# Where the split weights begin in their buffers: one start for both parts, or one for each

## The chip, the cores and the metric

The kernel runs on one core of a Trainium2 chip. The metric is the device time of one execution in microseconds. Before the change it is 2129.86 us, the median of three runs (2129.07 to 2129.96).

## The reference

The reference computes a decoder trunk of two layers on 256 tokens of 2048 features, in float32. Layer 0 mixes tokens by MoBA attention (16 heads of 128; with 256 tokens there is one block of keys, so this is plain causal attention), layer 1 by multi-head latent attention (low-rank queries and keys/values, a shared rotary key). Each mixer is followed by a gated feed-forward part with a causal convolution of width 3 on the gate:

```python
def conv_glu_ffn(h, w_gate, w_up, conv_w, conv_b, w_down):
    g = h @ w_gate                                # 2048 -> 5632
    g = causal_depthwise_conv(g, conv_w, width=3) + conv_b
    return (jax.nn.silu(g) * (h @ w_up)) @ w_down # 5632 -> 2048

for i in range(2):
    x = x + mixer_i(rms_norm(x, attn_norm[i]))
    x = x + conv_glu_ffn(rms_norm(x, ffn_norm[i]), ...)
```

The weights are some 387 MB of float32; each is used once.

## The kernel before

**Tiling.** All weights are laid out on the host in the order of their use, as 370 units of four pieces; a piece is 128 partitions x 512 columns (288 in one projection). Each float32 operand is split into a high part in the type fp32r and a low part, what is left of it, and a product is made of three fp32r products: high x high, high x low, low x high. The pieces are consumed in 1480 steps, called quanta, one piece each.

There are two ways to use a piece:

- *By token* (`tok_major`, L238 to L240): the activations' columns are loaded into TensorE as weights, and the piece is streamed, 512 columns at a time, six matmuls a piece. This is used for the q, k and v projections of layer 0 (units 0 to 47, in four groups of twelve, one group for four heads, called the heads below) and for most projections of layer 1 (units 200 to 221).
- *By feature* (`feat_major`, L255 to L257): the piece is loaded into TensorE, 128 columns at a time, and 256 tokens of activations are streamed, twelve matmuls a piece, in triples. L255 is high weights x high activations, L256 high weights x low activations, L257 low weights x high activations. This is used for both output projections (units 48 to 63 and 222 to 237), gate/up and down of layer 0 (64 to 151 and 152 to 195), the first projection of layer 1 (196 to 199), and gate/up and down of layer 1 (238 to 325 and 326 to 369).

**Splitting.** `Stream.split` takes a raw piece that DMA has brought, lets ScalarE copy it into a buffer `whi` (L99) and VectorE subtract that copy from the raw piece into a buffer `wlo` (L100). There are five buffers of either kind, used in turn. A buffer has 512 + 64 floats in each partition, that is 2304 bytes, nine times 256. The part need not begin at the buffer's first byte: `starts(u, j)` gives, for piece j of unit u, at which float the high part begins and at which the low part. Eight floats are 32 bytes.

```python
b, c = self.starts(u, j)
hi = self.part_pool.tile([P, 512 + ROOM], F32R, name="whi")[:, b : b + 512]
lo = self.part_pool.tile([P, 512 + ROOM], F32R, name="wlo")[:, c : c + 512]
```

Before the change, high and low part of a piece begin at the same place: at 32 bytes where pieces are used by token, at 96 bytes where they are used by feature, and at 80 bytes in the first piece of certain units (`entries`) of the feature-major stages: every eighth unit in gate/up, every eleventh in down, and single ones in the output projections and in unit 197. The activations' tile `h` begins 32 bytes into its buffer.

**Order.** The order of the work is written out by hand: each quantum's matmuls, and a table of side work (norms, evacuations, attention heads) that is put in behind given quanta. TensorE's queue is therefore one fixed list. In gate/up and down it holds nothing but L255, L256 and L257. In the first unit of each gate/up, two pieces of work of the norm stand between the matmuls, behind the unit's third and fourth piece: the sums (`column_rstd`, L320) and two transposes that spread the result over the partitions (`spread_rows`, L330). Attention's transposes (L443, L503) and scores (L467) stand between matmuls in the heads, in layer 1's projections and in the output projections.

Of the kernel before, what the change touches and what calls it, by code (L numbers as in the profile page):

```python
# [45 lines left out]

ROOM = 64

BY_TOKEN, BY_FEATURE, ENTRY = 8, 24, 20

H_START = 8

# [58 lines left out]
def trunk(ctx: ExitStack, tc: tile.TileContext, a, out):  # L111
# [38 lines left out]
    units += units_of("ffn_down1")  # L150
    def starts(u, j):

        if u < 48 or 200 <= u < 222:
            return BY_TOKEN, BY_TOKEN
        b = ENTRY if j == 0 and u in entries else BY_FEATURE
        return b, b


    entries = {52, 56, 60, 197, 224, 226, 228, 230, 234}
    for first_unit, n, every in ((65, 87, 8), (152, 44, 11), (239, 87, 8), (326, 44, 11)):  # L160
        entries |= set(range(first_unit, first_unit + n, every))
    assert len(units) == 370
    ws = Stream(nc, raw_pool, part_pool, units, starts)


# [930 lines left out]
```

## Time and profile before

| what | value |
|---|---|
| median of three runs | 2129.86 us |
| profiled execution | 2129.42 us, its span 2127.6 us |
| TensorE busy | 2119.6 us, 100% of the span |
| VectorE, ScalarE busy | 1388.7 us (65%), 1140.9 us (54%) |
| granted clock | 1.0 |
| HBM | 387.01 MB read, 183 GB/s |

In a timeline, each row has the start of an instruction, its duration (that of a matmul is modelled, and matmuls overlap), the engine, the line, and out<-in. The distance between two starts is what TensorE really spends on a matmul. In a table of windows each row is one stretch of the span: the busy time and, in brackets, the number of instructions of each engine that lie in it or reach into it.

### The profile page before, as it was taken

The numbers are of one execution on the slowest core, as the hardware profiler recorded it, in microseconds if no ns is written. First come the engines' busy times: TensorE is split into PE (matmuls) and PEld (weight loads), VectorE is DVE, ScalarE is ACT, GpSimd is POOL, SyncE is SP. The second block draws the span as 40 slices with busy tenths as digits, with TensorE's granted clock in tenths as the row PEclk, the third lists the DMA queues.
The fourth block names the chain that finished last, engine by engine and source line by source line (L and its number), as shares of the span: only waits on it lengthen the run. The fifth ranks groups of instructions, "written<-read, shape, count | busy, mean of one in ns | idle before, by whom it ended". The sixth has DMA issues, their size and how long they took to land.

```text
span 2127.6 us, 42062 instructions
## 1 busy us (share of the span) xinstructions
PE 2119.6 (100%) x16683; PEld 2045.3 (96%) x16683; DVE 1388.7 (65%) x3035; ACT 1140.9 (54%) x2207; POOL 45.6 (2%) x37
## 2 busy tenths in 40 slices
PE   9999999999999999999999999999999999999999
PEld 7888889999999999999999789999999999999999
DVE  6776666766667666655556885766666666654554
ACT  6555555555555555555556675655555555544443
POOL 0000000000000000000000210000000000000000
PEclk9999999999999999999999999999999999999999
DMA  7455445555555555555555433555555555555553
GB/s 268 159 178 178 158 164 194 193 189 194 199 196 187 193 198 198 198 187 192 197 181 186 144 115 139 187 191 191 186 183 194 179 193 184 185 197 193 202 186 129
DMA packets 59381, 391.81 MB, mean 184 GB/s; under 512 B 6960, under 2 KB 10032, under 8 KB 13232
## 3 DMA queue, kind: packets, MB, share of 16 engines
q1 hardware_dynamic: 59040, 389.10, 51.4%
q8 instruction: 130, 2.13, 0.4%
q14 instruction: 67, 0.55, 0.1%
q10 hardware_dynamic: 144, 0.04, 0.0%
HBM read 387.01 MB, written 2.10 MB: 183 GB/s over the span
## 4 chain that ended last, share of the span: by engine, by line
PE 98%; DVE 1%; issue 0%; ACT 0%; POOL 0%; DMA 0%; SPq 0%; POOLq 0%; ACTq 0%
PE acc L256 26%; PE acc L255 26%; PE acc L257 26%; PE acc L239 5%; PE acc L238 5%; PE acc L240 5%; PE sc L467 1%; PE tp L443 1%; PE sc L514 1%; PE tp L503 0%; PE sc L470 0%; PE sc L515 0%; DVE wlo L100 0%; DVE junk L373 0%; POOL hr L386 0%
## 5 line engine op out<-in xcount | busy, mean ns | idle before, releaser
L100 DVE TENSOR_TENSOR wlo<-raw,whi 128x512 fp32r<-128x512 f32 (+1 forms) x1480 | 999.9, 683 | 436.4 <-ACT whi L99 434.4
L99 ACT CAST whi<-raw 128x512 fp32r<-128x512 f32 (+1 forms) x1480 | 878.7, 614 | 477.8 <-PE acc L256 328.0
L255 PE MATMUL acc<-h,whi 128*128 128x256 f32 x2880 | 802.7, 279 | 0.0
L256 PE MATMUL acc<-h,whi 128*128 128x256 f32 x2880 | 802.3, 279 | 0.0
L257 PE MATMUL acc<-h,wlo 128*128 128x256 f32 x2880 | 802.1, 279 | 0.0
L255 PEld LDWEIGHTS acc<-h,whi 128*128 128x128 f32 x2880 | 546.5, 190 | 0.0
L257 PEld LDWEIGHTS acc<-h,wlo 128*128 128x128 f32 x2880 | 540.8, 188 | 0.0
L256 PEld LDWEIGHTS acc<-h,whi 128*128 128x128 f32 x2880 | 540.7, 188 | 0.0
L256 PE MATMUL acc<-a,whi 128*128 128x256 f32 x1408 | 392.3, 279 | 0.0
L255 PE MATMUL acc<-a,whi 128*128 128x256 f32 x1408 | 392.3, 279 | 0.0
L257 PE MATMUL acc<-a,wlo 128*128 128x256 f32 x1408 | 392.2, 279 | 0.0
L255 PEld LDWEIGHTS acc<-a,whi 128*128 128x128 f32 x1408 | 267.3, 190 | 0.0
L257 PEld LDWEIGHTS acc<-a,wlo 128*128 128x128 f32 x1408 | 264.4, 188 | 0.0
L256 PEld LDWEIGHTS acc<-a,whi 128*128 128x128 f32 x1408 | 264.3, 188 | 0.0
L238 PE MATMUL acc<-whi,h 128*128 128x512 f32 (+1 forms) x448 | 176.0, 393 | 0.5 <-ACT whi L99 0.5
L239 PE MATMUL acc<-wlo,h 128*128 128x512 f32 (+1 forms) x448 | 170.0, 379 | 0.1
L240 PE MATMUL acc<-whi,h 128*128 128x512 f32 (+1 forms) x448 | 169.6, 379 | 0.0
L255 PE MATMUL acc<-oT,whi 128*128 128x256 f32 x512 | 145.0, 283 | 0.0
L256 PE MATMUL acc<-oT,whi 128*128 128x256 f32 x512 | 141.8, 277 | 0.0
L257 PE MATMUL acc<-oT,wlo 128*128 128x256 f32 x512 | 141.7, 277 | 0.0
L669 DVE TENSOR_TENSOR g<-acc,rstd_b 128x256 f32<-128x256 f32 x88 | 37.4, 425 | 131.0 <-PE acc L257 128.1
L676 ACT ACTIVATE c<-g,par 128x256 f32<-128x256 f32 x88 | 53.1, 603 | 110.2 <-DVE g L669 110.2
(146 smaller groups left out, 1737.5 us busy)
## 6 DMA issues: line engine op xcount, KB each, us to landing
raw<-in_ffn_gu SPq DMA_DIRECT2D x176, 1024.0 KB, 4.8
raw<-in_ffn_down SPq DMA_DIRECT2D x88, 1024.0 KB, 4.8
raw<-in_moba_wk SPq DMA_DIRECT2D x16, 1024.0 KB, 4.9
raw<-in_moba_wv SPq DMA_DIRECT2D x16, 1024.0 KB, 4.8
raw<-in_moba_wo SPq DMA_DIRECT2D x16, 1024.0 KB, 4.8
raw<-in_mla_wo SPq DMA_DIRECT2D x16, 1024.0 KB, 4.9
raw<-in_moba_wq SPq DMA_DIRECT2D x13, 1024.0 KB, 4.8
raw<-in_mla_wkv_a SPq DMA_DIRECT2D x8, 576.0 KB, 3.8
```

What stands on the lines that cost most here:

```text
L99: self.nc.scalar.copy(hi[:, :n], w)
L100: self.nc.vector.tensor_tensor(lo[:, :n], w, hi[:, :n].bitcast(F32), op=ALU.subtract)
L238: mm(o, hi, t_hi[:, :n], start=kt == 0, stop=False)
L239: mm(o, hi, t_lo[:, :n], start=False, stop=False)
L240: mm(o, lo, t_hi[:, :n], start=False, stop=kt == k_last)
L255: mm(o, w_hi, src[:, kt, :S], start=first and k == 0, stop=False, skip_group_check=True)
L256: mm(o, w_hi, src[:, kt, S:], start=False, stop=False, skip_group_check=True)
L257: mm(o, w_lo, src[:, kt, :S], start=False, stop=kt == k_last, skip_group_check=True)
L443: nc.tensor.transpose(tp[:, (i * NT + t) * P : (i * NT + t + 1) * P], flat[:, t, c : c + P], ident)
L467: mm(o, qT[:, i, q0 : q0 + P], kT[:, i, :n], start=True, stop=self.rope is None)
L669: nc.vector.tensor_tensor(self.g[:, 2:], self.gate["acc"][:, :S], self.norm.rstd_b, op=ALU.mult)
L676: nc.scalar.activation(self.c, self.g[:, 2:], AF.Identity, bias=par[:, cb : cb + 1], scale=self.cw(2))
```

## The change

The high part of a feature-major piece stays at 96 bytes; its low part moves from 96 to 224 bytes. The pieces at 80 bytes are gone: the first pieces of the `entries` units are now like all others. In the heads of layer 0, the four groups of twelve units get a pair each: (32, 32) as before in the first, (32, 160) in the second, (224, 96) in the third and (96, 224) in the fourth. Layer 1's token-major pieces stay at (32, 32). The order of instructions is the same on all engines.

```diff
-BY_TOKEN, BY_FEATURE, ENTRY = 8, 24, 20
+BY_TOKEN, BY_FEATURE = (8, 8), (24, 56)
+BY_HEADS = ((8, 8), (8, 40), (56, 24), (24, 56))
...
     def starts(u, j):
 
-        if u < 48 or 200 <= u < 222:
-            return BY_TOKEN, BY_TOKEN
-        b = ENTRY if j == 0 and u in entries else BY_FEATURE
-        return b, b
-
-
-    entries = {52, 56, 60, 197, 224, 226, 228, 230, 234}
-    for first_unit, n, every in ((65, 87, 8), (152, 44, 11), (239, 87, 8), (326, 44, 11)):
-        entries |= set(range(first_unit, first_unit + n, every))
+        if u < 48:
+            return BY_HEADS[u // 12]
+        return BY_TOKEN if 200 <= u < 222 else BY_FEATURE
+
```

## The prediction

> **What bounds the kernel now.** I read the page first (busy time, clock, chain), then the busy time of each engine by stage, then TensorE's timeline where two stages begin.
>
> ```profile
> span 2127.6 us, 42062 instructions
> PE 2119.6 (100%) x16683; PEld 2045.3 (96%) x16683; DVE 1388.7 (65%) x3035; ACT 1140.9 (54%) x2207; POOL 45.6 (2%) x37
> PE 98%; DVE 1%; issue 0%; ACT 0%; POOL 0%; DMA 0%; SPq 0%; POOLq 0%; ACTq 0%
> ```
>
> TensorE is busy all the time and is 98% of the chain that ended last. VectorE and ScalarE have a third and more to spare. So only two things can move the time: how many matmuls there are (the change leaves that alone) and how far apart their starts lie.
>
> The stages that matter are gate/up and down of both layers, in which nothing but weight matmuls runs. These are windows, gate/up from the norm's transposes on, down from its first matmul (busy time and count of PE, PEld, DVE, ACT, POOL, then clock, DMA share, GB/s): gate/up and down of layer 0, gate/up and down of layer 1, and heads 4 to 15 of layer 0.
>
> ```profile
> 398.95:872.90 473.95, 473.95 (x4178) 473.95 (x4177) 329.51 (x610) 254.57 (x482) 0.00 (x0) 1.00 0.55 195
> 872.90:1112.47 239.57, 239.57 (x2114) 239.57 (x2113) 135.74 (x223) 120.61 (x206) 0.00 (x0) 1.00 0.55 194
> 1382.97:1874.96 491.99, 491.99 (x4178) 491.99 (x4178) 329.68 (x610) 260.80 (x482) 0.00 (x0) 1.00 0.53 188
> 1874.96:2123.62 248.66, 248.66 (x2114) 248.66 (x2112) 124.09 (x190) 106.93 (x173) 0.00 (x0) 1.00 0.51 182
> 74.96:300.63 225.67, 225.26 (x1066) 187.08 (x1064) 153.08 (x477) 122.09 (x257) 11.80 (x6) 1.00 0.48 171
> ```
>
> Gate/up from there on is 348 pieces of 12 matmuls, 4176 in all (the count takes in the ones that the edges cut). They take 473.95 us in layer 0 and 491.99 in layer 1; the 176 pieces of down, 2112 matmuls, take 239.57 and 248.66. Code, shapes, starts and pieces at 80 are the same in both layers, TensorE never idles, the clock is 1.00. So there are **two prices** for one and the same matmul: 473.95 / 4176 = 113.5 ns, which I call fast, and 491.99 / 4176 = 117.8 ns, slow. Which one holds is settled at this entry and then lasts for all 524 pieces, through the change from gate/up to down. The entry of layer 0:
>
> ```profile
> 398.76 0.43 PE L330 MATMUL tp<-ident,rstd 128*128 128x128 f32 x2
> 398.95 0.36 PE L255 MATMUL acc<-h,whi 128*128 128x256 f32 x1
> 399.15 0.28 PE L256 MATMUL acc<-h,whi 128*128 128x256 f32 x1
> 399.27 0.28 PE L257 MATMUL acc<-h,wlo 128*128 128x256 f32 x1
> ...
> 400.44 0.28 PE L255 MATMUL acc<-h,whi 128*128 128x256 f32 x1
> ...
> 400.79 0.28 PE L255 MATMUL acc<-h,whi 128*128 128x256 f32 x1
> ```
>
> and of layer 1:
>
> ```profile
> 1382.97 0.36 PE L255 MATMUL acc<-h,whi 128*128 128x256 f32 x1
> 1383.17 0.28 PE L256 MATMUL acc<-h,whi 128*128 128x256 f32 x1
> 1383.29 0.28 PE L257 MATMUL acc<-h,wlo 128*128 128x256 f32 x1
> ...
> 1384.47 0.28 PE L255 MATMUL acc<-h,whi 128*128 128x256 f32 x1
> ...
> 1384.82 0.28 PE L255 MATMUL acc<-h,whi 128*128 128x256 f32 x1
> ```
>
> Read the first column. In both, the norm's two transposes (L330) break the stream, the first gap is 0.20, and the first piece, which is one at 80 bytes, takes 1.49 and 1.50 us. The next triple takes 0.35 us in both, and from there layer 0 goes on at 0.34 a triple (its window) and layer 1 stays at 0.354 a triple (its window). From the second matmul to the piece's end it is 1.29 us (399.15 to 400.44) against 1.30 (1383.17 to 1384.47): that 0.01 us is all in which the two entries differ.
>
> **The change, part by part.** The order of instructions is the same on all five engines, so no wait, queue or DMA moves. What changes is where reads of the weights begin.
>
> 1. *Pieces at 80 go.* At the fast price one costs, at the start of layer 0's down,
>
> ```profile
> 872.90 0.28 PE L255 MATMUL acc<-a,whi 128*128 128x256 f32 x1
> ...
> 874.31 0.28 PE L255 MATMUL acc<-a,whi 128*128 128x256 f32 x1
> ```
>
> 1.41 us for 12 matmuls against 12 x 0.1133 = 1.36: 0.05 us dearer, and it falls back to fast at once. Layer 0's gate/up holds 11 of them (0.55 us), its down 4 (0.20), the other feature-major stages 7 amid fast ones (0.35). Without them the fast price is (473.95 - 0.55) / 4176 = 113.4 ns, the entry's stall in it. At the slow price none of the 14 later pieces at 80 of layer 1 brought the fast price back, so nothing is lost there by taking them out.
>
> 2. *What the entry then looks like.* The first piece behind L330 becomes an ordinary one. For ordinary pieces (both parts at 96) that start behind transposes or sums there are 24 (in the output projections, unit 196 and the first unit of gate/up) whose first gap is 0.20 or 0.21. I followed the gaps of each: 20 settle at 0.113, most of them within four matmuls, and 4 stay at 0.118. The first of the 24, one of the four (from its second matmul), and the last (likewise):
>
> ```profile
> 302.48 0.37 PE L255 MATMUL acc<-oT,whi 128*128 128x256 f32 x1
> 302.68 0.28 PE L256 MATMUL acc<-oT,whi 128*128 128x256 f32 x1
> ...
> 303.60 0.28 PE L255 MATMUL acc<-oT,whi 128*128 128x256 f32 x1
> ```
>
> ```profile
> 1293.05 0.28 PE L256 MATMUL acc<-oT,whi 128*128 128x256 f32 x1
> ...
> 1293.99 0.28 PE L255 MATMUL acc<-oT,whi 128*128 128x256 f32 x1
> ```
>
> ```profile
> 1381.44 0.28 PE L256 MATMUL acc<-h,whi 128*128 128x256 f32 x1
> ...
> 1382.13 0.28 PE L256 MATMUL acc<-h,whi 128*128 128x256 f32 x1
> ```
>
> From the second matmul on, eight gaps take 0.92 us in the first (302.68 to 303.60), eight 0.94 in the second (1293.05 to 1293.99), six 0.69 in the third (1381.44 to 1382.13): fast, slow, fast. All three of the 24 that read the norm's output are fast, the last of them two microseconds ahead of layer 1's slow entry. If an ordinary piece opens the stage, fast is the likely state of each layer, at 20 in 24 if the low parts' new place does no harm. Layer 1 at the fast price: gate/up 491.99 - 473.40 = 18.6 us less; down, whose window holds 2111 gaps, 248.66 - 2111 x 0.1133 = 9.4 less.
>
> 3. *Low parts 128 bytes further on.* No row has a high and a low part at different starts, so this price is unknown. What bears on it: a buffer is 2304 bytes, nine times 256, so consecutive pieces alternate by 256 bytes modulo 512, and the settled spacing in the windows does not; a move by 256 is free. A move by 16 (the pieces at 80) costs 0.05 us a piece. 128 lies between. Its ends: nothing (0.1133 a matmul), and every feature-major piece at the 1.41 of the piece at 80, which is also the slow price. I take nothing, since 128 keeps the place within 128 bytes, and 80 does not keep the place within 64; the other end stays as a rival.
>
> 4. *Heads of layer 0.* In these stages the weights are the streamed side (512 columns), and in the last three groups the pairs move one part or both. Here a stall is followed by some five unsettled gaps:
>
> ```profile
> 294.25 0.39 PE L239 MATMUL acc<-wlo,h 128*128 128x512 f32 x1
> ...
> 295.40 0.39 PE L238 MATMUL acc<-whi,h 128*128 128x512 f32 x1
> ```
>
> five gaps in 1.15 us, 0.230 each, against 0.2267 settled (1.36 us for a piece of six, as in 12 matmuls of 256). These groups have 144 x 6 = 864 such matmuls and 53 stalls. Ends: all unsettled gaps vanish, 53 x 5 x 0.0033 = 0.9 us less; or none ever settles, 864 x 0.0033 = 2.9 us more. I take 0, between them. VectorE and ScalarE write the parts at other places too; they are busy for 153 and 122 of these 226 us, and that spare time hides a small change; uncovered, 1% on their writes would be a microsecond or two.
>
> *What is late next.* Layer 1 at layer 0's pace asks for weights at layer 0's 195 GB/s, and for splitting at its 329.5 us of VectorE in 474; layer 0 shows TensorE without a gap at that pace.
>
> *Sum.* 18.6 + 9.4 + 0.55 + 0.20 + 0.35 = 29.1 us. The profiled execution took 2129.42 us, 0.44 under the median of 2129.86; from there 2100.3, and for the median **2100.8 us**.
>
> **Rivals.**
> - *Both layers slow (other side).* The low parts' new start keeps the two reads in each other's way, or both entries fall among the 4 of 24. Now 645 of the 1200 feature-major pieces run fast; at 1.413 instead of 1.36 that is 645 x 0.053 = 34 us more, less the 1.1 us of pieces at 80: 2163 us. For it: the slow price is stable, nothing in layer 1 ended it in 740 us, and the pieces that would shake it are gone. Against: 20 of 24. It decides once more than half of the pieces that are now fast are slow while layer 1 stays as it is.
> - *One layer each.* Layer 1 stays slow and only the pieces at 80 are saved: 2129.9 - 1.1 = 2128.8. With the layers swapped, 27 us lost and 28 won, the same to a microsecond.
> - *A price of its own.* If moving one part alone makes each gap the dearest settled one in rows above (0.12), 14400 x 0.12 = 1728 us stands against now 645 x 1.36 + 555 x 1.413 = 1661: 67 more, 2197. Some price between fast and slow, 0.1156 in all gaps, ends at about 2132.
> - *Starts do not matter at all*, and the prices come of stalls alone: with the same order, both layers stay as they are, 2129.9. Against it: 1.41 for a piece at 80. The Trainium skill, "TensorE: Matmul & The Clock Gate", section "Step-by-step: what each phase is for", has a rule of this kind: TensorE reads SBUF through two independent ports, so loading the next weights takes no bandwidth from the running matmul. By that rule the change is worth nothing; the trace disagrees with it as far as the piece at 80 goes.
>
> **How the numbers follow.** That the low parts' new place does no harm I hold at 0.67. Within it 20 of 24 stand for fast at each entry, and as both entries are alike their outcomes go together: both fast 0.50, one fast 0.11, both slow 0.06. With harm: the slow price everywhere 0.20, so both slow comes to 0.26; a price of its own 0.11. Starts without effect: 0.02. 2100.8 is that of the first case, whose own range is 2098 to 2105 (heads -0.9 to +2.9, and some ten slow pieces of the output stages won or as many more lost, 0.5). The range of all reaches from 2097 to the second large case, 2164, and leaves out some 0.1 above it. Faster by over 0.2% (4.3 us, about what a measurement tells from no change) 0.50, within 0.2% 0.13, slower 0.37.
>
> **What would show it.** Right: the windows of gate/up at 473.4 us in both layers, down at 239.4, gaps of 0.11 from the fifth matmul behind the L330 of each layer. Step 1: no triple of 0.35 at the start of down. Step 3 wrong: a settled triple that is neither 0.340 nor 0.353. Step 4: other gaps than 0.227 in the settled heads. The prediction falls if a layer's window shows 492, or if the price is a third one.

## The result, and the profile after

The changed kernel takes 2102.91 us (median of four runs, 2102.62 to 2103.16), beside 2129.66 for the kernel before; the ratio is 0.9875, its 95% interval 0.9858 to 0.9892. The profiled execution took 2103.16 us. Its page, span and busy time:

```profile
span 2101.3 us, 42062 instructions
PE 2093.2 (100%) x16683; PEld 2016.4 (96%) x16683; DVE 1389.1 (66%) x3035; ACT 1135.1 (54%) x2207; POOL 45.6 (2%) x37
```

TensorE is as busy as before, and does the same number of instructions in 26.3 us less. The windows of the changed kernel answer to those shown of before: gate/up and down of layer 0, gate/up and down of layer 1, and then the last three groups of the heads one by one.

```profile
401.61:875.01 473.40, 473.40 (x4178) 473.40 (x4178) 329.77 (x610) 254.53 (x482) 0.00 (x0) 1.00 0.55 195
875.01:1114.37 239.36, 239.36 (x2114) 239.36 (x2113) 135.83 (x223) 120.59 (x206) 0.00 (x0) 1.00 0.54 194
1384.73:1858.10 473.37, 473.37 (x4178) 473.37 (x4178) 329.81 (x610) 254.62 (x482) 0.00 (x0) 1.00 0.55 195
1858.12:2097.37 239.25, 239.25 (x2114) 239.25 (x2112) 123.96 (x191) 107.20 (x173) 0.00 (x0) 1.00 0.54 189
75.13:153.23 78.10, 77.69 (x366) 63.51 (x364) 55.06 (x177) 41.63 (x89) 4.02 (x2) 1.00 0.48 169
153.23:228.23 75.00, 75.00 (x349) 61.61 (x348) 49.16 (x151) 39.99 (x83) 3.89 (x2) 1.00 0.46 169
228.23:303.34 75.11, 75.11 (x353) 62.03 (x352) 49.02 (x151) 40.72 (x87) 3.89 (x2) 1.00 0.48 169
```

Layer 1 now runs gate/up at layer 0's pace: 473.37 us where it took 491.99, and down in 239.25 where it took 248.66. Layer 0 has lost what its pieces at 80 cost, 0.55 and 0.21. The three groups of heads take 228.21 us together. The same three windows of the kernel before:

```profile
74.96:152.05 77.09, 76.69 (x365) 63.49 (x364) 54.99 (x177) 41.52 (x89) 4.02 (x2) 1.00 0.48 172
152.05:226.10 74.05, 74.05 (x349) 61.57 (x348) 49.10 (x151) 39.85 (x83) 3.89 (x2) 1.00 0.48 171
226.10:300.63 74.53, 74.53 (x354) 62.02 (x352) 48.99 (x151) 40.72 (x87) 3.89 (x2) 1.00 0.47 170
```

225.67 us: here the change has lost 2.54. The timeline of the changed kernel where layer 1's gate/up begins (its matmul lines have numbers four smaller, L251 is what was L255):

```profile
1384.56 0.43 PE L326 MATMUL tp<-ident,rstd 128*128 128x128 f32 x2
1384.75 0.36 PE L251 MATMUL acc<-h,whi 128*128 128x256 f32 x1
1384.95 0.28 PE L252 MATMUL acc<-h,whi 128*128 128x256 f32 x1
1385.07 0.28 PE L253 MATMUL acc<-h,wlo 128*128 128x256 f32 x1
...
1386.20 0.28 PE L251 MATMUL acc<-h,whi 128*128 128x256 f32 x1
```

From the third matmul on, ten gaps take 1.13 us, 0.113 each: the stage is at the fast price after two matmuls.

### The profile page after: what moved, and what is told of

Its sections match the earlier page's. It is cut to its first block, busy times and chain, and to the rows that moved or that the text cites. A ratio compares the mean times of both kernels' runs of the same rounds, so it can differ in the third digit from the quotient of the medians.

```text
span 2101.3 us, 42062 instructions
## 1 busy us (share of the span) xinstructions
PE 2093.2 (100%) x16683; PEld 2016.4 (96%) x16683; DVE 1389.1 (66%) x3035; ACT 1135.1 (54%) x2207; POOL 45.6 (2%) x37
## 4 chain that ended last, share of the span: by engine, by line
PE 98%; DVE 1%; issue 0%; ACT 0%; POOL 0%; DMA 0%; SPq 0%; POOLq 0%; ACTq 0%
PE acc L251 26%; PE acc L253 26%; PE acc L252 26%; PE acc L235 5%; PE acc L234 5%; PE acc L236 5%; PE sc L463 1%; PE tp L439 1%; PE sc L510 1%; PE tp L499 0%; PE sc L466 0%; PE sc L511 0%; DVE wlo L101 0%; DVE junk L369 0%; POOL hr L382 0%
## 5 line engine op out<-in xcount | busy, mean ns | idle before, releaser
L251 PE MATMUL acc<-h,whi 128*128 128x256 f32 x2880 | 795.3, 276 | 0.0
L251 PEld LDWEIGHTS acc<-h,whi 128*128 128x128 f32 x2880 | 540.7, 188 | 0.0
L251 PE MATMUL acc<-a,whi 128*128 128x256 f32 x1408 | 388.6, 276 | 0.0
L251 PEld LDWEIGHTS acc<-a,whi 128*128 128x128 f32 x1408 | 264.3, 188 | 0.0
L251 PE MATMUL acc<-oT,whi 128*128 128x256 f32 x512 | 144.9, 283 | 0.0
```

Source lines behind the costliest of these rows:

```text
L251: mm(o, w_hi, src[:, kt, :S], start=first and k == 0, stop=False, skip_group_check=True)
```

## The experiments

Three theories stood at the start. P: with the low part 128 bytes behind the high one the slow price cannot last, whatever an entry looks like. O: the piece at 80 that opened layer 1's gate/up put it at the slow price, and the low part's place is neutral. L: every entry is a draw, and this change drew well. The first four kernels ran on one chip, the next four on another, the next three and then the last on a third. One thing has to be known of the kernel before to read them: its runs beside the experiments ended at two times, near 2102 and near 2129 us, two of 19 at the lower one beside the first four kernels, 12 of 15 beside the next four, five of 11 beside the next three, and the one run beside the last. So the price of layer 1 is drawn anew in each execution, and the 2129.86 given for it is one of two results. Against a run of the kernel before near 2102 us the change's 2102.91 is no gain at all: what the change can win is that no run ends at 2129.

**No pieces at 80, both parts at 96.** The change with its new pairs taken out.

```diff
-BY_TOKEN, BY_FEATURE = (8, 8), (24, 56)
-BY_HEADS = ((8, 8), (8, 40), (56, 24), (24, 56))
+BY_TOKEN, BY_FEATURE = (8, 8), (24, 24)
+BY_HEADS = ((8, 8),) * 4
```

> Both parts at 96 in all feature-major pieces, no pieces at 80, heads at (32, 32): the change without its new pair and without the heads' pairs. Theory P (the distance of 128 bytes between the parts makes the slow price unstable) expects that the slow price still holds somewhere: each of the two entries is a draw, some pieces of the output projections stay at 1.413 us, and if layer 1 draws slow the time is 2128 to 2129 us. Theory O (the piece at 80 that opened layer 1's gate/up put it in the slow price, the low parts' place is neutral) expects gate/up at 473.4 us in both layers and 2100 to 2101 us.

Six of eight runs ended between 2100.0 and 2101.0 us, two at 2127.9 and 2128.1; in the profile both layers are fast. I ran it again, on another chip:

> Both parts at 96 without pieces at 80, once more with more runs: the entries are draws, so the runs should again end at two times, near 2100.5 and near 2128, while the pair (96, 224) in the same call has one time alone. If all runs of this kernel end at 2100.5 as well, the new pair buys nothing over taking the pieces at 80 out.

Two of six runs at 2100.1 and 2100.3, four between 2127.6 and 2128.5. This time the profiled execution was one of the latter. Its windows of gate/up in both layers, and its entry into layer 1:

```profile
399.09:872.47 473.38, 473.38 (x4179) 473.38 (x4177) 329.77 (x610) 254.52 (x482) 0.00 (x0) 1.00 0.55 195
1382.08:1874.00 491.92, 491.92 (x4178) 491.92 (x4177) 329.94 (x610) 260.51 (x482) 0.00 (x0) 1.00 0.53 188
```

```profile
1382.08 0.36 PE L251 MATMUL acc<-h,whi 128*128 128x256 f32 x1
1382.28 0.28 PE L252 MATMUL acc<-h,whi 128*128 128x256 f32 x1
...
1383.46 0.28 PE L253 MATMUL acc<-h,wlo 128*128 128x256 f32 x1
```

Ten gaps of 0.118 from the second matmul on, with an ordinary piece at the opening and no piece at 80 in the whole kernel. So the slow price needs no piece at 80: theory O falls as the whole cause. Eight of 14 runs were fast, against the 20 of 24 that I had read from single pieces. Whether the pieces at 80 shift the odds stays open: on the first chip six of eight runs without them were fast, and two of 19 of the kernel before; on the third chip two of six, and five of 11.

**The new pair with the pieces at 80 kept.**

```diff
         b = ENTRY if j == 0 and u in entries else BY_FEATURE
-        return b, b
+        return (b, b) if b == ENTRY else (24, 56)
```

> The kernel before with ordinary feature-major pieces at (96, 224), its 39 pieces at (80, 80) kept, heads at (32, 32). Theory P expects the fast price in both layers in spite of the opening piece at 80: gate/up near 474 us in both layers, and 39 pieces each some 0.05 us dearer, so 2100.4 + 2 = 2102 us. Theory O expects layer 1's gate/up at 492 us again, since the piece at 80 opens it: 2129 us.

2102.26 us (two runs, 2101.8 and 2102.7). Gate/up of layer 0 and of layer 1:

```profile
398.54:872.49 473.95, 473.95 (x4178) 473.95 (x4177) 329.79 (x610) 254.56 (x482) 0.00 (x0) 1.00 0.55 195
1382.63:1856.59 473.96, 473.96 (x4179) 473.96 (x4178) 329.81 (x610) 254.65 (x482) 0.00 (x0) 1.00 0.55 195
```

Both layers are fast although a piece at 80 opens both; the 0.56 us more than 473.40 are the eleven pieces at 80. Theory P had 2102.

**The opening pieces at 80 alone taken out**, the other 37 kept, both parts at 96.

```diff
-    for first_unit, n, every in ((65, 87, 8), (152, 44, 11), (239, 87, 8), (326, 44, 11)):
+    for first_unit, n, every in ((73, 79, 8), (152, 44, 11), (247, 79, 8), (326, 44, 11)):
```

> The kernel before without the two pieces at 80 that open gate/up behind the norm's transposes, the other 37 kept, both parts at 96. If the opening piece at 80 is what puts layer 1 in the slow price, layer 1 is fast in most runs, as without any pieces at 80: 2101.5 us, gate/up at 474.0 in both. If another piece at 80 does it, or the entry's timing alone, it stays at 2129.

All eight runs ended between 2101.5 and 2103.1, gate/up 473.91 in both layers. But the kernel before ended near 2102 in 12 of 15 runs on that chip, so this does not tell the opening piece from chance.

**The change without the heads' pairs.**

```diff
-BY_HEADS = ((8, 8), (8, 40), (56, 24), (24, 56))
+BY_HEADS = ((8, 8),) * 4
```

> The change with the heads of layer 0 left at (32, 32). In the trace after, groups 2, 3 and 4 of the heads take 78.1, 75.0 and 75.1 us against 77.1, 74.05 and 74.5 before, 2.5 us more. If the pairs themselves cost that, the groups go back to 77.1, 74.05 and 74.5, and the time is 2100.4 us, 2.5 below the changed kernel, with both gate/up stages still at 473.4. If the feature-major fast price depends on when the heads end, one gate/up stage may fall to 492 us, and the time is 2128 us.

2100.62 us (four runs, 2100.32 to 2100.89; ratio to before 0.9886, 0.9813 to 0.9959). The three groups of heads and gate/up of both layers:

```profile
75.23:152.30 77.07, 76.67 (x365) 63.49 (x364) 55.01 (x177) 41.53 (x89) 4.02 (x2) 1.00 0.48 172
152.30:226.36 74.06, 74.06 (x350) 61.58 (x349) 49.14 (x151) 39.88 (x83) 3.89 (x2) 1.00 0.49 171
226.36:300.88 74.52, 74.52 (x353) 62.01 (x352) 49.02 (x151) 40.72 (x87) 3.90 (x2) 1.00 0.48 170
399.15:872.55 473.40, 473.40 (x4178) 473.40 (x4178) 329.75 (x610) 254.50 (x482) 0.00 (x0) 1.00 0.55 195
1382.26:1855.66 473.40, 473.40 (x4179) 473.40 (x4177) 329.79 (x610) 254.61 (x482) 0.00 (x0) 1.00 0.55 195
```

The heads are back at 225.65 us and the rest is as in the changed kernel. This version ends below both kernels: 2.3 us under the change's median, and its four runs lie wholly below the change's four. They were not taken side by side, but the heads' windows, 225.65 against 228.21 us, account for the difference.

**The heads' pairs alone**, on the kernel before.

```diff
-        if u < 48 or 200 <= u < 222:
+        if u < 48:
+            return ((8, 8), (8, 40), (56, 24), (24, 56))[u // 12]
+        if 200 <= u < 222:
             return BY_TOKEN, BY_TOKEN
```

> The kernel before with the heads' four pairs alone. The heads should cost 2.5 us more than before, 2132.4 us, if feature-major stages stay as they are. If which price an entry takes depends on small differences in timing ahead of it, either layer may change: 27 us less or more.

2131.93 us, eight runs from 2131.1 to 2132.3. The heads took 78.06, 75.01 and 75.10 us, 2.5 more than before, and layer 1 stayed slow in all eight. The pairs cost what the changed kernel's windows say.

**Equal starts in the heads**, each group another one, with (96, 224) in the feature-major stages.

```diff
-BY_HEADS = ((8, 8), (8, 40), (56, 24), (24, 56))
+BY_HEADS = ((8, 8), (24, 24), (40, 40), (56, 56))
```

> Feature-major pieces as in the change, the heads' groups at (32, 32), (96, 96), (160, 160) and (224, 224). The groups took 77.1, 74.05 and 74.5 us at (32, 32), and 78.1, 75.0 and 75.1 at the change's pairs. If any move away from (32, 32) costs a group something, each of the last three is dearer; if only parts that differ cost, they are as at (32, 32); a group below that would be a better start for the heads. As to the feature-major stages, theory P expects gate/up at 473.4 us and every run within 3 us of the others.

The three groups:

```profile
74.24:151.63 77.39, 77.00 (x365) 63.55 (x364) 55.02 (x177) 41.56 (x89) 4.01 (x2) 1.00 0.47 171
151.63:226.99 75.36, 75.36 (x349) 61.71 (x348) 49.14 (x151) 39.98 (x83) 3.88 (x2) 1.00 0.47 168
226.99:302.96 75.97, 75.97 (x353) 62.13 (x352) 49.12 (x151) 40.92 (x87) 3.89 (x2) 1.00 0.48 167
```

0.3, 1.3 and 1.4 us more than at (32, 32): any move costs, equal parts too, and no start tried in a group beat 32. The kernel's six runs lie between 2102.8 and 2104.7, so by their times all had fast feature-major stages.

**Other places of the parts.** Four kernels like the one with the heads at (32, 32), each with another feature-major pair in place of (24, 56): (56, 24), (56, 56), (24, 40) and (8, 40).

> Feature-major pieces at (224, 96): the pair of the change turned round, no pieces at 80, heads at (32, 32). If the distance of 128 bytes between the parts is what makes every entry settle fast, this settles as (96, 224) does: gate/up 473.4 us in both layers, every piece behind a break fast at its end, 2100.5 us in every run. If it is the low part's own place that counts, some pieces behind breaks stay at 1.413 us and single runs may end at 2128.

> Both parts at 224: both moved by 128 bytes, so no distance between them, no pieces at 80, heads at (32, 32). If the distance counts, this behaves as (96, 96) did: about a quarter of the pieces behind breaks stay at 1.413 us, and some runs have a layer at 492 us (2128). If the low part's place at 224 counts, all settle fast and all runs are at 2100.5.

> Feature-major pieces at (96, 160): the low part 64 bytes behind the high part instead of 128, no pieces at 80, heads at (32, 32). After (224, 224) at 2162.9 and (32, 160) at 2182.4, the place of each part against the activations counts, not the distance alone. If a low part may lie anywhere so long as the high one is at 96, this is at 2100.5; if the low part has a good place only at 224 or 96, the triple settles at another sum and the time lies between 2130 and 2165.

> Feature-major pieces at (32, 160): distance 128 at another place, 64 bytes ahead of the change's, no pieces at 80, heads at (32, 32). If the distance alone counts, as (96, 224): 473.4 us in both layers, all settle, 2100.5. If the place relative to the activations counts as well, the settled spacing or the share that settles differs; ends 2100 and 2163.

Gate/up of layer 0 and of layer 1 at (224, 224), then at (96, 160), then at (32, 160) with down of layer 0 between them:

```profile
401.92:893.84 491.92, 491.92 (x4178) 491.92 (x4178) 330.04 (x610) 260.77 (x482) 0.00 (x0) 1.00 0.53 188
1416.46:1908.38 491.92, 491.92 (x4178) 491.92 (x4177) 330.04 (x610) 260.82 (x482) 0.00 (x0) 1.00 0.53 188
```

```profile
402.43:896.21 493.78, 493.78 (x4179) 493.78 (x4177) 329.92 (x610) 261.00 (x482) 0.00 (x0) 1.00 0.53 187
1420.30:1914.08 493.78, 493.78 (x4178) 493.78 (x4177) 329.98 (x610) 261.06 (x482) 0.00 (x0) 1.00 0.53 187
```

```profile
403.51:901.00 497.49, 497.49 (x4179) 497.49 (x4177) 329.96 (x610) 261.55 (x482) 0.00 (x0) 1.00 0.52 186
901.00:1152.56 251.56, 251.56 (x2114) 251.56 (x2113) 136.73 (x222) 120.53 (x206) 0.00 (x0) 1.00 0.52 185
1427.87:1925.36 497.49, 497.49 (x4179) 497.49 (x4177) 330.03 (x610) 261.57 (x482) 0.00 (x0) 1.00 0.52 186
```

Together with the pairs above. The third column is gate/up divided by 4176; the fourth counts, in one profile (in two at (96, 96)), the 34 pieces that begin behind other work, called the breaks below, and of them those whose eleventh gap is 115 ns or less:

| pair, bytes | gate/up, us | ns a matmul | settled fast | runs, us |
|---|---|---|---|---|
| (96, 96) | 473.38 or 491.92 | 113.4 or 117.8 | 25 and 24 of 34 | 2100.0 to 2101.0, or 2127.6 to 2128.5 |
| (96, 224) | 473.40 | 113.4 | 34 of 34 | 2100.3 to 2100.9 |
| (224, 96) | 473.39 | 113.4 | 17 of 34 | 2101.2 to 2102.4, one 2136.3 |
| (224, 224) | 491.92 | 117.8 | 2 of 34 | 2162.8, 2163.0 |
| (96, 160) | 493.78 | 118.2 | 0 of 34 | 2169.4, 2169.5 |
| (32, 160) | 497.49 | 119.1 | 0 of 34 | 2182.1, 2182.6 |

Three of the four new pairs came out as neither of the two cases in their expectations: (224, 224) was to draw or to be fast and is slow in both runs, (32, 160) was to end at 2163 at most and ends at 2182, and (96, 160) was to end at 2100.5 or by 2165 and ends at 2169.5. The distance alone does not explain the prices: three pairs have 128 bytes between the parts, one always fast, one mostly, one never. Two pairs have none, one a draw and one always slow. Each part's own place counts. At (96, 224) alone every break settles within its piece (in all three profiled kernels that have this pair and no pieces at 80), and by their times all 16 runs of kernels with their ordinary pieces at this pair are fast in both layers (four of the change, and four, two and six of the experiments), pieces at 80 or not. Theory P holds for this pair, and not for 128 bytes as such; L is refuted for it and holds for (96, 96).

**The activations moved too.** To see against what a place is measured, h begins at 160 bytes in place of 32, and the pair is (160, 32): against h, modulo 256, this is (32, 160) once more, while the activations that down reads stay where they were.

```diff
-H_START = 8
+H_START = 40
-BY_TOKEN, BY_FEATURE = (8, 8), (24, 56)
+BY_TOKEN, BY_FEATURE = (8, 8), (40, 8)
```

> The activations' tile h begins at 160 bytes instead of 32, the feature-major pairs are (160, 32), no pieces at 80. Against h, modulo 256, the parts lie as (32, 160) lay against h at 32: the high part at the same place, the low part 128 away. If what counts is the place against the streamed activations, gate/up, which streams h, takes 497.5 us in both layers as with (32, 160), and down, whose activations did not move, has another price than 251.6. If the place in memory alone counts, gate/up and down have one price a matmul, whatever it is: the ratio of gate/up (4176 matmuls) to down of layer 0 (2112) is 1.977. The heads of layer 0 and the first projections read h too, so their times move as well.

Gate/up and down of layer 0:

```profile
407.27:904.76 497.49, 497.49 (x4179) 497.49 (x4178) 329.92 (x610) 261.50 (x482) 0.00 (x0) 1.00 0.52 186
904.76:1154.68 249.92, 249.92 (x2115) 249.92 (x2113) 136.73 (x222) 120.42 (x206) 0.00 (x0) 1.00 0.53 186
```

In this one run, of 2182.51 us, gate/up is at 497.49 to the hundredth, down at 249.92 instead of 251.56; one price a matmul, as at (32, 160), would have made it 497.49 x 2112 / 4176 = 251.6. So what counts is where the loaded weights lie against the streamed activations, modulo 256 bytes. The heads read h as well and moved too: their last three groups took 228.96 us, against 225.67 in the kernel before. The rule that I set against the change from the Trainium skill ("TensorE: Matmul & The Clock Gate", "Step-by-step: what each phase is for"), that loading weights takes nothing from the running matmul's reads, is not borne out here: the same matmul takes 113.4 ns at (96, 224) and 119.1 at (32, 160), by nothing but the two reads' relative start.

## Why the prediction was right, point by point

The time, 2102.91, lies 2.1 us above the 2100.8 that I gave, and the case that I held likeliest, both layers fast, is what happened. In part this was luck: the reasons given for steps 2 and 3 are not borne out, and their terms came out all the same.

- *Two prices, settled at the entry.* Right, and sharper than I had it: the price is drawn in each execution, since the kernel before ends at two times.
- *Step 1, the pieces at 80.* Right: gate/up of layer 0 was to be 473.40 and is 473.40; down 239.37 and is 239.36. The 0.35 us of the other feature-major stages came as 0.19: from the heads' end to gate/up of layer 0, 98.32 us before and 98.27 after; from the end of down to gate/up of layer 1, 270.50 and 270.36.
- *Step 2, layer 1 at the fast price.* Its size is right: 18.6 and 9.4 us were expected, and 491.99 - 473.37 = 18.6 and 248.66 - 239.25 = 9.4 came (2111 x 0.1133 as printed gives 9.5; 9.4 is with 1.36 / 12 not rounded). Its reason is not. I put it down to the ordinary piece at the opening, at 20 in 24; with ordinary pieces and the old pair only eight of 14 runs were fast. It is the new pair that settled all 34 pieces.
- *Step 3, the low parts' place.* The argument of this step failed, although its term, nothing, came true for the pair of the change. I argued that 128 bytes are free because 256 are. Moves by 64 or 128 bytes are not free: (224, 224) costs 62 us against (96, 224), (96, 160) 69, (32, 160) 82. That the change's pair is the best of the six is luck: nothing in the rows of before could tell it. The end that I kept as a rival, every feature-major piece at 1.413 and 2163 us, is what (224, 224) takes: 2162.9.
- *Step 4, the heads.* The mis-sized term: 0 was taken, 2.54 us measured, within the ends (-0.9 to +2.9) and near the one at which a group never settles. It is more than the whole miss of 2.1 us; with the heads left alone the kernel takes 2100.62 against 2100.8. It lies in the spacing, not in VectorE's and ScalarE's writes: in the traces' gaps under 260 ns of these groups, 811 in either kernel, what goes beyond 226.7 ns each adds up to 1.4 us before and 3.7 after, 2.4 of the 2.54.
- *The rivals.* One layer fast is, by their times, what the old pair gives in six of 14 runs without the pieces at 80 (one of them has a profile). A price of its own exists, at two other pairs. Starts without effect is refuted by the last experiment above all.

What stays open: why kernels at (96, 96) draw fast so much more often in one set of runs than in another, and what the chip and the pieces at 80 have to do with it; what made one run at (224, 96) end at 2136.3, since no profile shows such an execution; and what makes 256 bytes the period. A low part at 32 bytes beside a high part at 96 was not tried.

## What to carry to other kernels

When TensorE is the bound and the same loop shows two spacings in one trace, compare the starts of the loaded and the streamed operand modulo 256 bytes before looking for a wait: a start costs nothing to change, and here it was worth between nothing and 82 us. Look at how the spacing settles behind each break, not only at its mean: a place at which every break settles is worth more than one that is as fast when it is lucky. And choose starts for each way of using an operand separately, since (96, 224), the best pair where the weights are loaded, cost the one group of heads that had it 0.58 us (75.11 against 74.53), where they are streamed.

## What the runs showed of the hardware

- A 128-column fp32r weight load and a 256-column matmul repeat every 113.4, 117.8, 118.2 or 119.1 ns at the same granted clock of 1.00, by the relative start of the two reads and, at (96, 96), by the draw; the relation repeats after 256 bytes (497.49 us with the low part 128 bytes ahead of h's start or 128 behind it) and not after 128 (both parts at 224 take 491.92 in both layers, both at 96 only sometimes).
- At one pair, (96, 96), two spacings are stable, and an execution can keep either for the 740 us from the start of layer 1's gate/up to the end.
- The spread of a kernel's time between executions can come from this draw, with TensorE busy throughout and the clock at 1.00 in the profiles of both kinds: 2100.1 and 2128.5 us for the same program on the same chip.
